# Gated MLP of a decoder layer: two leading pairs of plain products, and the last two down groups added in SBUF

## The chip, the cores and the metric

One core of a Trainium2 chip runs the kernel. The metric is the device time of one execution in microseconds (us), as a median over several executions. A change of about 0.2%, 5 us, is what a measurement of this kernel can tell from no change. An execution with the hardware profiler on gives the trace that is read here.

## The reference

The kernel computes one layer of a hybrid decoder on 2048 tokens of width 1024: three causal mixers with one input and one output projection, then a gated MLP, then a per-layer embedding with a gate, then a norm. The change touches the MLP alone:

```python
def conv_ffn(h, w_up, conv_w, w_down):          # h = rmsnorm(x): 2048 x 1024
    gu = causal_dwconv(h @ w_up, conv_w)        # w_up 1024 x 5632, taps of width 3
    g, u = jnp.split(gu, 2, axis=-1)            # 2 x 2816
    return (jax.nn.silu(g) * u) @ w_down        # w_down 2816 x 1024

x = x + conv_ffn(rmsnorm(x, norm_ffn_gain[i]), ffn_w_up[i], ffn_conv_w[i], ffn_w_down[i])
```

## The kernel before

**Halves, chunks, pairs.** The tokens are worked in two halves (`hf`) of 1024, a half in two chunks of 512, which is the width of one matmul. Activations lie with channels on the 128 partitions and tokens along the free side. The 2816 gate and 2816 up channels make `NJ` = 22 pairs `j` of 128 + 128 channels. Every operand of a matmul is split into a high and a low part (`split`, line 253: ACT copies the high part with rounding, DVE subtracts it from the source), and one product of a weight block with an activation block takes three matmuls (`mm3`, line 261: high x high, high x low, low x high; lines 262, 263, 264 of the profile).

**Products.** `prod` (line 847) multiplies one weight quarter (128 output channels, half of the input channels, so four blocks) with one activation set `X[i]`: 4 x 3 = 12 matmuls of 512 columns. `X[1]` and `X[2]` are the lower and the upper half of the channels of chunk 0, `X[3]` the upper half of chunk 1, `X[5]` chunk 1 minus chunk 0 of the lower half, and `X[6]`, `X[7]`, `X[4]` further differences. With them a pair (gate and up, two chunks, two channel halves: eight plain products) is had from seven products in the manner of Strassen and Winograd; its weights are sums of quarters that `up_jobs` (line 152) forms on DVE. `h2_first` (line 777) makes `X[1]` and `X[2]`, `h2_second` (line 786) the others, in steps between which products stand; eight of its subtractions run on POOL (lines 803 and 808).

**The lead.** `up_first` (line 881) works pair 0 with eight plain products, because the sums for the others aren't there yet: gate and up with `X[1]`, then `X[2]`, then `X[5]` and `X[3]`. The last four go to the two halves of one PSUM tile, `pbc`, of two banks. `up(j)` (line 919) works each further pair with seven products, and in between finishes pair `j - 1`: the depthwise convolution of width 3 (`conv`, line 399: one ACT operation for the first tap, a DVE step for each further one), silu, the multiplication (`gu_mul`) and the split of the result (`gu_split`).

**Down.** `GROUPS` (line 99) holds ten groups of two pairs and then pairs 20 and 21 alone. `down_pair` (line 950) multiplies a group of two with its down weights, six matmuls to a tile, copies the result out of PSUM on ACT (line 961) and adds it to `xd` in DRAM by an accumulating transfer of POOL's queue (line 962). After the last such group `x` is loaded from `xd` (line 1003). `down_last` (line 966) works pair 20 and then pair 21: three matmuls to a tile of 128 channels and one chunk, and DVE adds the tile into `x` in SBUF (line 974); for pair 21 the sum is split at once (`xsplit`, line 947) for the gate products that follow. Pair 21's silu, last product, convolution and multiplication are issued ahead of pair 20's tiles, its split after the sixth.

**What sets the order.** Weights are split in the order of `wlist` (lines 209 to 226), some jobs ahead of their use (`w_get`, line 240; `w_mlp`, line 250). A scheduler then orders the instructions of each engine; an engine works its queue in that order and waits where an operand isn't there. Its dependencies go by whole tiles: a write to one half of a tile waits for a read of the other half. ACT and DVE share the work of all splits, so that a split can stand behind work that waits for something else. PSUM has four tiles of one bank (`sm`) and two of two banks (`mm`).

## Time and profile before

| | us |
|---|---|
| median of 3 runs | 2551.55 (2551.5 to 2554.44) |
| the profiled execution | 2548.32 |
| its span, first to last instruction | 2546.5 |
| PE busy in it | 2454.9 (96%) |
| DVE busy | 1613.4 (63%) |
| ACT busy | 1310.7 (51%) |
| POOL busy | 237.2 (9%) |

The profile names a group of instructions by its line, engine and operation, and by the tiles that it writes and reads: `pbc<-h,wt` is a matmul that writes the tile `pbc` from an activation tile `h` and a weight tile `wt`. An idle time stands with what ended it (`<-`). PE is the matmuls, PEld the loading of weights into the array, which runs beside them; PEclk is the clock granted to TensorE as a share of its full 2.4 GHz. A table of windows gives for each its limits, its length, the busy time and (x) the count of PE, PEld, DVE, ACT and POOL, then PEclk, the busy share of the DMA engines and GB/s. `pa`, `pb`, `pc` and `pbc` are the PSUM tiles of the up products, `pdn` those of the down products, `zg` and `zu` gate and up before the convolution, `gu` behind it, `ahi` and `alo` the split activation, `wt` a split weight.

The first half's MLP lies from about 465 to 1168 us of the span, the second half's from about 1715 to 2412 us.

### The profile page before, as it was taken

How to read it: one execution, taken by the hardware profiler on the slowest of the kernel's cores; microseconds unless marked ns; L12 is line 12 of the kernel's file. 1: busy time of each engine (PE TensorE's matmuls, PEld its weight loads, DVE VectorE, ACT ScalarE, POOL GpSimd, SP SyncE). 2: the span in 40 equal slices, each digit the busy share in tenths (PEclk: the TensorE clock that was granted, in tenths of full speed). 3: DMA queues.
4: the chain of work that ended last, by engine and by line, in shares of the span. 5: the costliest groups of instructions: out<-in, count | busy, mean ns of one | idle time of the engine just before them, and what ended most of it. 6: DMA issues, size and time to landing. Idle time of an engine off the chain costs nothing. (4 is left out here: it accounts for less than half of the span.)

```text
span 2546.5 us, 30816 instructions
## 1 busy us (share of the span) xinstructions
PE 2454.9 (96%) x12004; PEld 2020.1 (79%) x12004; DVE 1613.4 (63%) x2384; ACT 1310.7 (51%) x1778; POOL 237.2 (9%) x278
## 2 busy tenths in 40 slices
PE   6999999899999999999999999997999999999998
PEld 4887788678888888887888887785888888888788
DVE  6666565685556566558666656567666666655776
ACT  5444884365555545555344457634555555555453
POOL 2000001201111111110110000012111111111100
PEclk9999999899999999999999999998999999999999
DMA  3101114346565555573421111251555555556642
GB/s 136 42 26 34 42 58 164 122 120 138 132 137 135 140 124 124 127 195 116 149 92 34 34 34 54 79 189 39 124 129 136 133 125 128 133 130 136 177 149 92
DMA packets 121170, 280.71 MB, mean 110 GB/s; under 512 B 11840, under 2 KB 42176, under 8 KB 121024
## 3 DMA queue, kind: packets, MB, share of 16 engines
q0 software_dynamic: 31360, 113.26, 21.3%
q1 hardware_dynamic: 88656, 164.30, 19.9%
q8 instruction: 94, 1.54, 0.2%
q10 hardware_dynamic: 1008, 1.18, 0.2%
q14 instruction: 52, 0.43, 0.1%
HBM read 178.03 MB, written 100.66 MB: 109 GB/s over the span
## 5 line engine op out<-in xcount | busy, mean ns | idle before, releaser
L262 PE MATMUL pz<-h,wh 128*128 128x512 f32 x768 | 306.3, 399 | 9.5 <-ACT h L255 9.5
L263 PE MATMUL pz<-h,wh 128*128 128x512 f32 x768 | 302.0, 394 | 1.2 <-DVE h L256 0.8
L264 PE MATMUL pz<-h,wl 128*128 128x512 f32 x768 | 300.6, 392 | 0.0
L262 PE MATMUL pdn<-ahi,wt 128*128 128x512 f32 x704 | 277.7, 394 | 12.6 <-DVE x L974 11.0
L264 PE MATMUL pa<-h,wt 128*128 128x512 f32 x704 | 276.5, 393 | 6.8 <-DVE wt L256 6.8
L262 PE MATMUL pa<-h,wt 128*128 128x512 f32 x704 | 276.3, 393 | 3.3 <-ACT wt L255 1.8
L263 PE MATMUL pdn<-alo,wt 128*128 128x512 f32 x704 | 275.8, 392 | 0.0
L264 PE MATMUL pdn<-ahi,wt 128*128 128x512 f32 x704 | 275.6, 392 | 0.0
L263 PE MATMUL pa<-h,wt 128*128 128x512 f32 x704 | 275.6, 391 | 0.0
L961 ACT ACTIVATE st<-pdn 128x1024 f32<-128x1024 f32 x160 | 164.0, 1026 | 210.5 <-PE pdn L264 189.9
L256 DVE TENSOR_TENSOR wt<-s,wt 128x512 fp32r<-128x512 f32 x168 | 114.1, 688 | 218.0 <-ACT wt L255 217.8
L962 POOL DMA_DIRECT2D xd<-st x160 | 136.9, 856 | 1087.4 <-ACT st L961 1084.3
L262 PEld LDWEIGHTS pz<-h,wh 128*128 128x128 f32 x768 | 144.8, 189 | 40.7 <-ACT h L255 10.7
L263 PEld LDWEIGHTS pz<-h,wh 128*128 128x128 f32 x768 | 144.8, 189 | 33.0 <-DVE h L256 4.1
L262 PEld LDWEIGHTS pdn<-ahi,wt 128*128 128x128 f32 x704 | 133.2, 189 | 45.6 <-DVE x L974 13.9
L264 PEld LDWEIGHTS pz<-h,wl 128*128 128x128 f32 x768 | 144.8, 189 | 30.1 <-issue 0.3
L256 DVE TENSOR_TENSOR wl<-wr,wh 128x1024 fp32r<-128x1024 f32 x120 | 146.2, 1227 | 35.1 <-ACT wh L255 34.7
L264 PEld LDWEIGHTS pa<-h,wt 128*128 128x128 f32 x704 | 133.3, 189 | 35.3 <-DVE wt L256 7.7
L262 PEld LDWEIGHTS pa<-h,wt 128*128 128x128 f32 x704 | 133.1, 189 | 33.0 <-ACT wt L255 2.7
L264 PEld LDWEIGHTS pdn<-ahi,wt 128*128 128x128 f32 x704 | 133.2, 189 | 28.0
L263 PEld LDWEIGHTS pa<-h,wt 128*128 128x128 f32 x704 | 133.1, 189 | 27.6
L263 PEld LDWEIGHTS pdn<-alo,wt 128*128 128x128 f32 x704 | 133.3, 189 | 27.1
(271 smaller groups left out, 5170.0 us busy)
## 6 DMA issues: line engine op xcount, KB each, us to landing
xd<-st POOLq DMA_DIRECT2D x160, 512.0 KB, 6.1
wr<-in_w_up SPq DMA_DIRECT2D x176, 256.0 KB, 4.1
wr<-in_w_in SPq DMA_DIRECT2D x48, 512.0 KB, 3.7
q<-in_w_down SPq DMA_DIRECT2D x88, 256.0 KB, 3.4
wr<-in_w_pg SPq DMA_DIRECT2D x40, 512.0 KB, 4.5
wr<-in_w_out SPq DMA_DIRECT2D x32, 512.0 KB, 3.8
q<-in_w_up SPq DMA_DIRECT2D x42, 256.0 KB, 3.0
xr<-in_xT POOLq DMA_DIRECT2D x32, 256.0 KB, 3.9
```

The source lines that it names most:

```text
L256: last_split[:] = i, (eng or nc.vector).tensor_tensor(lo, src, hi.bitcast(F32), op=SUB)
L262: MM(ps, wk[0], rk[0], start=start, stop=False, **kw)
L263: MM(ps, wk[0], rk[1], start=False, stop=False, **kw)
L264: MM(ps, wk[1], rk[0], start=False, stop=stop, **kw)
L961: ACT(st, ps, AF.Copy)
L962: nc.gpsimd.dma_start(xd[m], st, accum_op=ADD)
```

## The change

Pair 1 is worked like pair 0, with eight plain products (`FIRST` = 2). The products of both are ordered by activation set: four with `X[1]`, four with `X[2]`, four with `X[5]`, four with `X[3]`; `w_get` orders their weights so. Pair 1's sums with `X[1]` and `X[2]` go to the two halves of a tile `pbc`, and each pair's sums with `X[5]` and `X[3]` to a tile of their own. `up` begins with pair 2 and there has no `X[4]` product of pair 1 to do. Pair 0's convolutions, silu, multiplication and split stand in `up_first`. POOL's eight subtractions per half go to DVE.

The groups are now eleven, all of two pairs. The first nine accumulate in DRAM as before; pairs 18 and 19 and pairs 20 and 21 go through `down_last` behind the last product, with six matmuls to a tile and the add into `x` on DVE. Pair 21's silu, convolution, multiplication and split are steps between the tiles of the group ahead of it. `x` is loaded from `xd` ahead of the last product, when nine groups have accumulated in place of ten.

```diff
@@ -96,7 +96,8 @@
     def ftile(name, dt=F32):
         return pools["ff"].tile([P, TH], dt, tag="ff", name=nm(name))
 
-    GROUPS = [[j, j + 1] for j in range(0, NJ - 2, 2)] + [[NJ - 2], [NJ - 1]]
+    GROUPS = [[j, j + 1] for j in range(0, NJ, 2)]
+    FIRST = 2
 
     def ple_chunks(last):
 
@@ -176,11 +177,11 @@
             TT(t[:, QS[1]], raws[a][:, QS[0]], raws[a][:, QS[1]], op=SUB)
             return one(t[:, QS[1]])
 
-        if j == 0:
-            return [(("f", hf, 0), load0, lambda: one(raws[a][:, QS[0]])),
-                    (("f", hf, 1), None, lambda: one(raws[a][:, QS[1]])),
-                    (("f", hf, 2), load1, lambda: one(raws[b][:, QS[1]])),
-                    (("f", hf, 3), None, lambda: one(raws[b][:, QS[0]]))]
+        if j < FIRST:
+            return [(("f", hf, j, 0), load0, lambda: one(raws[a][:, QS[0]])),
+                    (("f", hf, j, 1), None, lambda: one(raws[a][:, QS[1]])),
+                    (("f", hf, j, 2), load1, lambda: one(raws[b][:, QS[1]])),
+                    (("f", hf, j, 3), None, lambda: one(raws[b][:, QS[0]]))]
         return [((1, hf, j), load0, lambda: one(raws[a][:, QS[0]])),
                 ((5, hf, j), load1, s1),
                 ((6, hf, j), None, lambda: one(raws[s][:, QS[1]])),
@@ -210,12 +211,14 @@
     for hf in range(NH):
         wlist += [(("in", hf, m), lambda m=m: whole(kc(w_in[m]), t4)) for m in IN_UNITS]
         wlist += [(("out", hf, c, m), lambda m=m: whole(kc(w_out[m]), t4)) for c in range(NC) for m in range(KD)]
-        for j in range(NJ):
+        firsts = [up_jobs(hf, j) for j in range(FIRST)]
+        wlist += [job for i in (0, 2) for jobs in firsts for job in jobs[i : i + 2]]
+        for j in range(FIRST, NJ):
             jobs = up_jobs(hf, j)
-            if j > 1:
+            if j > FIRST:
                 jobs.insert(2, last_job(hf, j - 1))
             wlist += jobs
-            if j % 2 == 0 and j:
+            if j % 2 == 0 and j < NJ - 2:
                 wlist += down_jobs(hf, j // 2 - 1)
         wlist.append(last_job(hf, NJ - 1))
         for gi in range(len(GROUPS) - 2, len(GROUPS)):
@@ -800,15 +803,16 @@
             for q in range(KQ):
 
                 TT(h0[q], h1[KQ + q], h0[q], op=SUB)
-                nc.gpsimd.tensor_tensor(h1[q], h1[KQ + q], h1[q], op=SUB)
                 X[6][q] = split_chunk(h0[q], "h")
             yield
             for q in range(KQ):
 
-                nc.gpsimd.tensor_tensor(h0[KQ + q], h0[KQ + q], h0[q], op=SUB)
+                TT(h1[q], h1[KQ + q], h1[q], op=SUB)
                 X[7][q] = split_chunk(h1[q], "h")
             yield
             for q in range(KQ):
+
+                TT(h0[KQ + q], h0[KQ + q], h0[q], op=SUB)
                 X[4][q] = split_chunk(h0[KQ + q], "h")
 
         norms = [Norm(), Norm()]
@@ -880,34 +884,51 @@
 
         def up_first():
 
-            w0, w1 = w_get("f", hf, 0), w_get("f", hf, 1)
-            A, A2, BC = ps1(name="pa"), ps1(name="pa"), ps2("pbc")
-            zg, zu = ftile("zg"), ftile("zu")
-            prod(A, w0, X[1], True, False)
-            ACT(zg[:, C1], A, AF.Copy)
-            norms[1].rstd()
-            prod(A2, w1, X[1], True, False)
-            ACT(zu[:, C1], A2, AF.Copy)
-            h2 = h2_second(norms[1].bcast())
+            pairs = range(FIRST)
+            w = {}
+            sums0 = [[ps1(name="pa"), ps1(name="pa")], None]
+            for j in pairs:
+                zs[j, 0], zs[j, 1] = ftile("zg"), ftile("zu")
+            for j in pairs:
+                if j:
+                    t = ps2("pbc")
+                    sums0[j] = [t[:, C0], t[:, C1]]
+                for i in range(2):
+                    w[j, i] = w_get("f", hf, j, i)
+                    prod(sums0[j][i], w[j, i], X[1], True, False)
+                    ACT(zs[j, i][:, C1], sums0[j][i], AF.Copy)
+                    if j == 0 and i == 0:
+                        norms[1].rstd()
+                    if j == 0 and i == 1:
+                        h2 = h2_second(norms[1].bcast())
+                        next(h2)
+            for j in pairs:
+                for i in range(2):
+                    w[j, 2 + i] = w_get("f", hf, j, 2 + i, ahead=min(2, 3 - 2 * j - i))
+                    prod(sums0[j][i], w[j, 2 + i], X[2], False, True)
+                    ACT(zs[j, i][:, C0], sums0[j][i], AF.Copy)
+                next(h2)
+
+            sums1 = []
+            for j in pairs:
+                t = ps2("pbc")
+                sums1.append([t[:, C0], t[:, C1]])
+                for i in range(2):
+                    prod(sums1[j][i], w[j, i], X[5], True, False)
             next(h2)
-            w2 = w_get("f", hf, 2, ahead=1)
-            prod(A, w2, X[2], False, True)
-            ACT(zg[:, C0], A, AF.Copy)
-            next(h2)
-            w3 = w_get("f", hf, 3, ahead=0)
-            prod(A2, w3, X[2], False, True)
-            ACT(zu[:, C0], A2, AF.Copy)
-
-            prod(BC[:, C0], w0, X[5], True, False)
-            prod(BC[:, C1], w1, X[5], True, False)
-            next(h2)
-            prod(BC[:, C0], w2, X[3], False, True)
-            TT(zg[:, C1], zg[:, C1], BC[:, C0], op=ADD)
-            prod(BC[:, C1], w3, X[3], False, True)
-            TT(zu[:, C1], zu[:, C1], BC[:, C1], op=ADD)
-            zs[0, 0], zs[0, 1] = zg, zu
-            g_conv(0)
-            run(h2)
+            for j in pairs:
+                for i in range(2):
+                    prod(sums1[j][i], w[j, 2 + i], X[3], False, True)
+                    TT(zs[j, i][:, C1], zs[j, i][:, C1], sums1[j][i], op=ADD)
+                if j == 0:
+                    g_conv(0)
+                    u_conv(0)
+                    g_silu(0)
+                    gu_mul(0)
+                    gu_split(0)
+                    run(h2)
+                else:
+                    g_conv(1)
 
         banks = {}
 
@@ -922,11 +943,11 @@
             zg, zu = zs[j, 0], zs[j, 1] = ftile("zg"), ftile("zu")
             prod(A, w_mlp(1, hf, j), X[1], True, False)
             ACT(zg[:, C0], A, AF.Copy)
-            if j % 2 == 0 or j == 1:
+            if j % 2 == 0 or j == NJ - 1:
                 g_silu(j - 1)
             prod(B, w_mlp(5, hf, j), X[5], True, False)
             ACT(zu[:, C1], B, AF.Copy)
-            if j > 1:
+            if j > FIRST:
                 last_prod(j - 1)
             u_conv(j - 1)
             prod(A, w_mlp(6, hf, j), X[6], False, False)
@@ -965,17 +986,29 @@
 
         def down_last(gi, todo=None):
 
-            j = GROUPS[gi][0]
-            w = [w_mlp("d", hf, gi, i) for i in range(2)]
+            js = GROUPS[gi]
+            final = gi == len(GROUPS) - 1
+
+            def tile(m, c, w):
+                ps = ps1(name="pdn")
+                for i, j in enumerate(js):
+                    mm3(ps, wsl(hsl(w), m % 2 * 2 + i), [a[:, cks(c)] for a in acts[j]], i == 0, i == 1)
+                TT(x[m][:, cks(c)], x[m][:, cks(c)], ps, op=ADD)
+
+            if not final:
+                for m in range(KD):
+                    if m % 2 == 0:
+                        w = w_mlp("d", hf, gi, m // 2)
+                    for c in range(NC):
+                        tile(m, c, w)
+                    if todo:
+                        next(todo, None)
+                return
+            w = [w_mlp("d", hf, gi, i) for i in range(KD // 2)]
             for c in range(NC):
                 for m in range(KD):
-                    ps = ps1(name="pdn")
-                    mm3(ps, wsl(hsl(w[m // 4]), m % 4), [a[:, cks(c)] for a in acts[j]], True, True)
-                    TT(x[m][:, cks(c)], x[m][:, cks(c)], ps, op=ADD)
-                    if gi == len(GROUPS) - 1:
-                        xsplit(c, m)
-                    if todo and c == 0 and m == 5:
-                        todo()
+                    tile(m, c, w[m // 2])
+                    xsplit(c, m)
 
         def stats_steps():
             for c in range(NC):
@@ -991,22 +1024,29 @@
         up_first()
         nstats = []
         stats = iter(()) if last else stats_steps()
-        for j in range(1, NJ):
+        for j in range(FIRST, NJ):
             up(j)
-            if j > 1:
-                next(stats, None)
-            if j % 2 == 0:
+            next(stats, None)
+            if j % 2 == 0 and j < NJ - 2:
                 down_pair(j // 2 - 1, lambda: g_silu(j))
         run(stats)
+        j = NJ - 1
         for m in range(KD):
             x[m] = t4("x")
             nc.gpsimd.dma_start(x[m], xd[m])
-        j = NJ - 1
-        g_silu(j)
+
+        def last_steps():
+            g_silu(j)
+            yield
+            u_conv(j)
+            yield
+            yield
+            gu_mul(j)
+            yield
+            gu_split(j)
+
         last_prod(j)
-        u_conv(j)
-        gu_mul(j)
-        down_last(len(GROUPS) - 2, lambda: gu_split(j))
+        down_last(len(GROUPS) - 2, last_steps())
         down_last(len(GROUPS) - 1)
         ff.release()
 
```

How the change moves instructions is shown at three places, as they stand in each engine's queue. The number behind a name tells tiles of one kind apart; line numbers of the change are its own.

PE, first half, where the `X[5]` sums come in. Before, the `X[2]` products (`pa` with `wt_3518`) are done and `pbc_3523` begins:

```order
L264 MATMUL pa_3522<-h_3424,wt_3518 128x512
L262 MATMUL pbc_3523<-h_3576,wt_3444 128x512
L263 MATMUL pbc_3523<-h_3576,wt_3444 128x512
L264 MATMUL pbc_3523<-h_3576,wt_3444 128x512
L262 MATMUL pbc_3523<-h_3581,wt_3444 128x512
```

Now, from the sixth matmul on `X[5]` on (`pbc_3724`; `h_3577`, `h_3582` and `h_3587` are its first blocks), with `wt_3599`, `wt_3615` and `wt_3634` the weights for `X[2]` (`h_3363`):

```order
L267 MATMUL pbc_3724<-h_3582,wt_3444 128x512
L265 MATMUL pbc_3724<-h_3587,wt_3444 128x512
L265 MATMUL pa_3512<-h_3363,wt_3599 128x512
L266 MATMUL pa_3512<-h_3363,wt_3599 128x512
L266 MATMUL pbc_3724<-h_3587,wt_3444 128x512
L265 MATMUL pa_3513<-h_3363,wt_3615 128x512
L266 MATMUL pa_3513<-h_3363,wt_3615 128x512
L265 MATMUL pbc_3595<-h_3363,wt_3634 128x512
L267 MATMUL pa_3512<-h_3363,wt_3599 128x512
```

The last row is the first that takes the low part of a weight for `X[2]`; seven matmuls on `X[5]` stand ahead of the `X[2]` products, the rest of them behind.

ACT, first half, at the first weight of the first pair with seven products. Before, that is `wt_3746`, and the silu of pair 0 stands behind it:

```order
L255 ACTIVATE h_3733<-h_485_3270 128x512
L255 ACTIVATE h_3736<-h_485_3270 128x512
L255 ACTIVATE wt_3746<-wr_3743 128x512
L255 ACTIVATE wt_3755<-s_3752 128x512
L255 ACTIVATE wt_3758<-s_3752 128x512
L255 ACTIVATE wt_3761<-wr_3749 128x512
L867 ACT_TABLE_LOAD
L867 ACTIVATE gu_3706<-gu_3706 128x1024
```

Now it is `wt_3886`, for pair 2:

```order
L871 ACTIVATE gu_3816<-gu_3816 128x1024
L406 ACTIVATE gu_3821<-zu_3515,vt 128x1024
L406 ACTIVATE gu_3874<-zg_3516,vt 128x1024
L306 ACTIVATE sq_5844<-xs_5842 128x512
L306 ACTIVATE sq_6139<-xs_6137 128x512
L258 ACTIVATE ahi_3828<-gu_3816 128x1024
L258 ACTIVATE h_3833<-h_484_3269 128x512
L258 ACTIVATE h_3837<-h_484_3269 128x512
L258 ACTIVATE h_3841<-h_485_3270 128x512
L258 ACTIVATE h_3845<-h_485_3270 128x512
L258 ACTIVATE wt_3886<-wr_3883 128x512
```

The same place of DVE's queue in the change, where the multiplication of pair 0 (`gu_3816`) and the low parts stand:

```order
L922 TENSOR_TENSOR zu_3517<-zu_3517,pbc_3749 128x512
L410 SCALAR_TENSOR_TENSOR gu_3821<-zu_3515,vt,gu_3821 128x1022
L410 SCALAR_TENSOR_TENSOR gu_3874<-zg_3516,vt,gu_3874 128x1023
L878 TENSOR_TENSOR gu_3816<-gu_3816,gu_3821 128x1024
L410 SCALAR_TENSOR_TENSOR gu_3874<-zg_3516,vt,gu_3874 128x1022
L259 TENSOR_TENSOR alo_3829<-gu_3816,ahi_3828 128x1024
L259 TENSOR_TENSOR h_3833<-h_484_3269,h_3833 128x512
L259 TENSOR_TENSOR h_3837<-h_484_3269,h_3837 128x512
L259 TENSOR_TENSOR h_3841<-h_485_3270,h_3841 128x512
L259 TENSOR_TENSOR h_3845<-h_485_3270,h_3845 128x512
L259 TENSOR_TENSOR wt_3886<-wr_3883,wt_3886 128x512
```

The silu, multiplication and split of pair 0 moved ahead of the first weight of the next pair; the first row reads the last product of the lead, pair 1's `pbc_3749`.

PE, first half, the last down group. Before, two tiles of pair 21:

```order
L262 MATMUL pdn_8534<-ahi_8468,wt_8407 128x512
L263 MATMUL pdn_8534<-alo_8469,wt_8407 128x512
L264 MATMUL pdn_8534<-ahi_8468,wt_8407 128x512
L262 MATMUL pdn_8542<-ahi_8468,wt_8407 128x512
L263 MATMUL pdn_8542<-alo_8469,wt_8407 128x512
L264 MATMUL pdn_8542<-ahi_8468,wt_8407 128x512
```

Now, one tile of pairs 20 (`ahi_8193`) and 21 (`ahi_8372`), and the first matmul of the next:

```order
L265 MATMUL pdn_8448<-ahi_8193,wt_8315 128x512
L266 MATMUL pdn_8448<-alo_8194,wt_8315 128x512
L267 MATMUL pdn_8448<-ahi_8193,wt_8315 128x512
L265 MATMUL pdn_8448<-ahi_8372,wt_8315 128x512
L266 MATMUL pdn_8448<-alo_8373,wt_8315 128x512
L267 MATMUL pdn_8448<-ahi_8372,wt_8315 128x512
L265 MATMUL pdn_8459<-ahi_8193,wt_8315 128x512
```

A tile that DVE adds is now behind six matmuls in place of three.

## Rows read from the trace of the kernel before

**Rows 1.** The page, span and engine shares of the whole run.

```profile
span 2546.5 us, 30816 instructions
...
PE 2454.9 (96%) x12004; PEld 2020.1 (79%) x12004; DVE 1613.4 (63%) x2384; ACT 1310.7 (51%) x1778; POOL 237.2 (9%) x278
```

**Rows 2.** Waits of PE: line, what it waited for, us, times, longest.

```profile
PE pdn L262 <- DVE x L974: 11.0, 4, 4.9
...
PE pbc L262 <- DVE zg L905: 8.5, 2, 6.7
```

**Rows 3.** Windows: a steady stretch, the two leads, the two ends.

```profile
600.00:1090.00 490.00, 489.97 (x2167) 404.89 (x2166) 291.45 (x407) 257.27 (x350) 54.74 (x64) 1.00 0.57 132
487.00:556.10 69.10, 56.53 (x205) 42.86 (x205) 65.75 (x88) 39.80 (x64) 12.66 (x8) 0.85 0.24 77
1736.40:1805.10 68.70, 54.10 (x205) 40.97 (x205) 61.61 (x85) 35.68 (x54) 13.43 (x8) 0.88 0.13 41
1120.00:1180.00 60.00, 54.68 (x226) 43.40 (x226) 48.70 (x69) 30.06 (x41) 5.99 (x10) 0.94 0.53 166
2370.00:2432.00 62.00, 56.10 (x237) 45.30 (x235) 55.48 (x81) 30.50 (x42) 4.29 (x8) 0.94 0.42 145
```

**Rows 4.** Windows with the lower granted clock, same columns.

```profile
490.80:497.60 6.80, 5.92 (x13) 4.36 (x14) 6.80 (x9) 2.85 (x6) 3.78 (x3) 0.50 0.25 77
...
1767.50:1774.20 6.70, 6.09 (x14) 4.79 (x15) 3.92 (x7) 1.42 (x3) 0.00 (x0) 0.50 0.30 99
2395.60:2402.20 6.60, 4.14 (x10) 3.25 (x11) 6.53 (x9) 2.60 (x3) 0.00 (x0) 0.50 0.23 79
```

**Rows 5.** Timeline of PE, leads of both halves: start, duration, what, [idle before].

```profile
508.09 0.79 PE L262 MATMUL pbc<-h,wt 128*128 128x512 f32 x1 [1.78 <-DVE zg L905]
...
1756.97 0.79 PE L262 MATMUL pbc<-h,wt 128*128 128x512 f32 x1 [6.69 <-DVE zg L905]
...
1768.11 0.80 PE L264 MATMUL pa<-h,wt 128*128 128x512 f32 x1 [3.66 <-DVE wt L256]
```

**Rows 6.** Timeline of PE, end of the second half's MLP.

```profile
2398.06 0.80 PE L262 MATMUL pdn<-ahi,wt 128*128 128x512 f32 x1 [4.87 <-DVE x L974]
...
2409.43 0.50 PE L262 MATMUL pdn<-ahi,wt 128*128 128x512 f32 x1 [0.93 <-DVE x L974]
```

**Rows 7.** Timeline of DVE, lead of the first half.

```profile
491.73 1.28 DVE L256 TENSOR_TENSOR h<-h,h 128x512 fp32r<-128x512 f32 x2
...
495.58 3.46 DVE L256 TENSOR_TENSOR h<-h,h 128x512 fp32r<-128x512 f32 x2
...
512.61 0.69 DVE L907 TENSOR_TENSOR zu<-zu,pbc 128x512 f32<-128x512 f32 x1
...
514.41 4.29 DVE L256 TENSOR_TENSOR h<-h,h 128x512 fp32r<-128x512 f32 x7
...
528.80 1.28 DVE L407 SCALAR_TENSOR_TENSOR gu<-zu,vt,gu 128x1023 f32<-128x1023 f32 x1
...
532.43 1.22 DVE L874 TENSOR_TENSOR gu<-gu,gu 128x1024 f32<-128x1024 f32 x1
```

**Rows 8.** Timeline of DVE, lead of the second half.

```profile
1741.40 0.69 DVE L256 TENSOR_TENSOR h<-h,h 128x512 fp32r<-128x512 f32 x1
```

**Rows 9.** Timeline of ACT, lead of the first half and pair 2.

```profile
509.57 3.73 ACT L255 ACTIVATE h<-h 128x512 fp32r<-128x512 f32 x7
...
533.68 1.06 ACT L255 ACTIVATE ahi<-gu 128x1024 fp32r<-128x1024 f32 x1 [1.30 <-DVE gu L874]
534.64 0.61 ACT L255 ACTIVATE wt<-s 128x512 fp32r<-128x512 f32 x1
```

**Rows 10.** Timeline of DVE, end of the first half's MLP.

```profile
1162.89 2.35 DVE L256 TENSOR_TENSOR wl<-wr,wh 128x1024 fp32r<-128x1024 f32 x2
...
1166.96 1.89 DVE L256 TENSOR_TENSOR xs<-x,xs 128x512 fp32r<-128x512 f32 x3
1168.76 1.88 DVE L974 TENSOR_TENSOR x<-x,pdn 128x512 f32<-128x512 f32 x3
```

## Prediction

> **What bounds the kernel now.** I read the page first: TensorE (PE) is busy 96% of a span of 2546.5 us [rows 1], so the time is the PE's matmuls plus the stretches in which it stands still or runs slowly. A steady stretch gives the pitch: 2167 matmuls of 512 columns in 490 us, 0.2265 us each [rows 3]; nothing can be won there. So I looked for the stretches that the change touches and counted what they hold against that pitch. In the lead of the MLP, from the first product with the X5 sums to the first down product, 204 matmuls (the window's 205 holds one begun earlier) are worth 46.2 us and take 69.1 us in the first half, 68.7 us in the second: 22.9 and 22.5 us lost [rows 3]. At the end of the MLP, 225 of the 226 matmuls in a window of 60 us are worth 51.0 us and 235 in one of 62 us 53.2 us: 9.0 and 8.8 us lost [rows 3]. That is 63 us in all, the most that this change can work on.
>
> The waits of PE say what ends the idle time. At the end it is the add of a down product into x on VectorE (DVE), 11.0 us [rows 2], one wait of 4.87 us in the second half [rows 6]. In the lead the largest is the add that reads one half of the two-bank tile pbc, 8.5 us [rows 2], 6.69 us of it in the second half [rows 5]. The third loss is the clock: behind these waits the granted clock is 0.50, the lower level of 1.2 GHz, for stretches such as the three of 6.6 to 6.8 us shown [rows 4], and a matmul there costs twice the pitch. A wait thus also costs time behind it. PE resumes at 1768.11 and 2398.06 [rows 5, 6], in stretches that stay low up to 1774.2 and 2402.2 [rows 4]: 6.1 and 4.1 us of work at half rate, mean 5.1, so about 2.5 us lost per wait.
>
> **The lead, part by part.** Pair 1 gets eight products in place of seven: 12 more matmuls per half, +2.7 us; 216 are now worth 48.9 us. Three pair-1 weight sums and splits go, which only frees DVE and ScalarE (ACT).
>
> First wait, kept. The order puts seven matmuls on X5 (ten in the second half) ahead of the X2 products, and X2's weights are split only behind the last X5 split. Up to the first low part of a weight PE has 13 matmuls (14). In the first half it starts them at about 486.8; DVE ends its last X5 split at 491.73 + 1.28 = 493.0 [rows 7], and one split more (seven in 4.29 us: 0.60 each [rows 7]) makes 493.7 with the handoff. Loss 6.9 - 13 x 0.2265 = 4.0 us. Up to here the work is that of before, so the low clock from 490.8 to 497.6 [rows 4] stays: 3.9 us of work at half rate, 1.95 us. Second half: from 1736.2 to 1741.40 + 0.69 + 0.60 = 1742.7 [rows 8], 6.5 - 14 x 0.2265 = 3.3 us; there the clock held before, and I count nothing.
>
> Then PE has 83 matmuls on X2 and X5 before the first one on X3, some 19 us. DVE needs about 10 us for what X3 wants: four weight splits, four scalings, two subtractions, four splits. So the X3 waits of before vanish. The eight subtractions taken from POOL cost DVE 8 x 0.60 = 4.8 us per half, but two DVE splits beside POOL's subtractions took 3.46 us in place of 1.2 [rows 7]; that stretching goes. The rest of DVE's queue up to the first add of an X3 product is some 23 operations, 14 us: it gets there about when that product is done, 516 to 517 us. I cost the move at nothing; the cover is thin, and the first rival prices its absence.
>
> The half-tile wait stays in part: the last X3 product of pair 1 writes one half of a tile whose other half DVE must have read. PE now has another product between, so only the tail of an add and a convolution step is left. The nearest row, 1.78 us [rows 5], is the upper end, nothing the lower; I take 1.5 and 1.0 us. The Trainium skill (Perfetto Trace Analysis, Optimizing Tensor Performance, Matmuls) says that groups in different PSUM banks let the evacuation of one overlap the matmuls of the next; by that the two halves, a bank each, need not wait, and the sum would be 2.5 us lower. The trace disagrees for this code, 6.69 us [rows 5]: the dependency is on the tile.
>
> New wait, the heart of this sum. The order shows the first weight of pair 2 behind the high part of pair 0's activation and four X4 splits on ACT. That activation needs the whole of pair 0: once the last X3 product is done, DVE adds it (0.69), does two convolution steps (1.28 each; in the second half the queue has them elsewhere) and the multiplication (1.22) [rows 7]; then ACT makes the activation's high part (1.06), four splits (seven in 3.73: 0.53 each) and the weight (0.61) [rows 9]. Nothing else is left for PE. First half, with consecutive DVE steps at 1.20 and 0.4 us of handoffs: 0.4 + 0.6 + 1.2 + 1.2 + 1.2 + 1.06 + 2.1 + 0.6 = 8.4 us; second half without the two steps 6.0 us. The low part, behind DVE's own queue, comes about 0.9 us later: 9.3 and 6.9 us. Then the low clock, unseen for this place: 0 if it holds, 3.4 if all 6.8 us lie on work, 2.5 taken as above.
>
> Sum of the losses: 4.0 + 1.95 + 1.5 + 9.3 + 2.5 = 19.3 us, so the first down product starts at 486.8 + 48.9 + 19.3 = 555.0 against 556.1: **-1.1 us**. Second half: 3.3 + 1.0 + 6.9 + 2.5 = 13.7, 1736.2 + 48.9 + 13.7 = 1798.8 against 1805.1: **-6.3 us**. What the eight products win in the lead they nearly give back behind pair 0.
>
> **The end, part by part.** The matmuls stay the same in number. Before, the last two groups come three matmuls to a tile: a tile takes PE 0.68 us and DVE an add of 0.63 (three in 1.88), in the last pass also a split of 0.63 [rows 10]: 1.26 us, so DVE bound it, and pair 21's convolutions and splits stood in the same queue. Now a tile takes six matmuls, 1.36 us, the same DVE work: in the first pass half of DVE is free for pair 21, whose 21.7 us of cover replace 10.9; in the last pass 1.26 is below 1.36. The x loads no longer wait for the accumulations of pairs 18 and 19, which end in PSUM and are added straight; 8 evacuations on ACT and 8 stores per half go, off PE's path. What remains I bound by nothing and by the smallest wait there now, 0.93 us [rows 6], and take the upper. **-8.1 us** and **-7.9 us**.
>
> Sum: -1.1 - 6.3 - 8.1 - 7.9 = **-23.4 us**. The profiled execution took 2548.3 us (span 2546.5 and 1.8 around it), which gives 2524.9; the median of the runs shown is 2551.55, 3.2 us above it, and on that I forecast 2528 us. About 0.2%, 5 us, is what a measurement can tell from no change.
>
> **Rivals.**
> A: DVE becomes the bound of the lead. For it: DVE is busy 65.8 of 69.1 us there [rows 3] and meets PE with a margin of a microsecond. Against: the stretching beside POOL goes. If all eight subtractions fall on the path, 2 x 4.8 = 9.6 us come back: 2538 us. The Trainium skill (Perfetto Trace Analysis, Optimizing Scalar/DVE Operations) speaks for this rival: work may be offloaded to GpSimd where DVE is saturated, and the change does the reverse; it adds that the two share a read port so that it might not help, and the 3.46 us bears that out. Chance 0.12.
> B: the last pass is still DVE's. The weight splits of the next stage stand in that queue (two in 2.35 us [rows 10]); with three of them DVE's 16 tiles take 16 x 1.26 + 3.5 = 23.7 us against 21.7: 2 us per half, 2532 us. Chance 0.10.
> C, on the other side: the clock stays low between the two waits of the lead and behind them. Each matmul more at the low level costs 0.2265 us; from (23.4 + 5) / 2 / 0.2265 = 63 per half the kernel is slower, and with all 135 from 497.6 us up to the new wait it is 2528 + 2 x 135 x 0.2265 = 2589 us. For it: the new wait is the longest in the MLP. Against: the low stretches of waits up to 6.7 us end by themselves [rows 4, 5]. Chance 0.04.
> D: the new chain takes twice as long (DVE late, ACT held by statistics): 2 x 8 more, 2544, and with two further low stretches no change, 2549 us. Chance 0.05.
>
> **How the numbers follow.** Forecast 0.69, A 0.12, B 0.10, D 0.05, C 0.04. Faster 0.69 + 0.12 + 0.10 = 0.91, same 0.05, slower 0.04. The low end takes no low clock (-6.95), no half-tile wait (-2.5) and no rest at the end (-1.8): 2517. The high end holds A (2538) and the low clock at 3.4 behind each wait: 2540. C and D are left out.
>
> **What would show it.** Right: PE waits for pair 2's first weight split once per half, 6 to 9 us, with a granted clock of 0.50 behind it; the 6.69 us wait and the add waits of the last groups are gone; no DVE split of h takes over 1.2 us. Wrong: end losses over 3 us per half (B), a wait of the first X3 add for DVE's own queue (A), low stretches over 7 us (C), a lead of more than 69 us.

## The result, and the profile after

The changed kernel takes 2520.97 us, the median of four runs (2518.2 to 2523.93), against 2551.53 us for four runs of the kernel before (2547.7 to 2554.44) beside it: ratio 0.988, 95% interval 0.9864 to 0.9896. The forecast was 2528 us, in a range of 2517 to 2540. It was faster, as forecast, by about 30.6 us by the medians where the working gave 23.4.

The profiled execution after the change took 2518.2 us, with a span of 2516.4 us. The line of its page with the busy times, and its waits of PE, which answer to [rows 1, 2]:

```profile
PE 2445.4 (97%) x12028; PEld 2017.6 (80%) x12028; DVE 1599.2 (64%) x2384; ACT 1292.0 (51%) x1756; POOL 197.4 (8%) x246
```

```profile
PE pa L265 <- ACT wt L258: 13.8, 3, 8.0
...
PE pbc L265 <- DVE zg L922: 2.0, 2, 1.2
```

The columns are what PE waited for, us in all, times, longest. The waits of a down product for an add into x (11.0 us before) do not occur at all; the wait for the half tile of pbc has gone from 8.5 to 2.0 us; and the wait for a split weight on ACT, 13.8 us, is the new one that the prediction was built around.

The windows of the two leads and the two ends after the change answer to [rows 3] (length, busy us and count of each engine, granted clock of PE, DMA share, GB/s):

```profile
484.00:552.30 68.30, 56.54 (x219) 44.10 (x218) 61.81 (x94) 40.11 (x63) 0.00 (x0) 0.88 0.25 79
1721.90:1784.70 62.80, 54.58 (x220) 42.10 (x219) 56.41 (x86) 33.82 (x52) 0.00 (x0) 0.95 0.13 40
1100.00:1160.40 60.40, 60.40 (x267) 49.72 (x267) 52.55 (x74) 27.18 (x39) 2.85 (x6) 1.00 0.42 149
2326.60:2388.70 62.10, 62.00 (x274) 51.00 (x274) 54.30 (x82) 29.38 (x43) 4.19 (x8) 1.00 0.43 153
```

The two lead windows also hold two or three matmuls that stand ahead of the lead. Counted as before, from the first product with the X5 sums (484.26 and 1722.36 us) to the first down product (552.26 and 1784.69), a lead holds 216 matmuls, worth 48.9 us at 0.2265 us each, and takes 68.0 and 62.3 us: 19.1 and 13.4 us are lost, where 22.9 and 22.5 were lost before. Both end windows lose nothing: 267 matmuls are worth 60.5 us and stand in 60.4, at a granted clock of 1.00, where 9.0 and 8.8 us were lost before.

The chain behind the new wait: PE's timeline in both halves (start, us, what, [idle before, releaser]), then DVE's and ACT's in the first half.

```profile
521.68 0.50 PE L265 MATMUL pbc<-h,wt 128*128 128x512 f32 x1 [1.19 <-DVE zg L922]
532.69 0.80 PE L265 MATMUL pa<-h,wt 128*128 128x512 f32 x1 [7.99 <-ACT wt L258]
...
1756.47 0.50 PE L265 MATMUL pbc<-h,wt 128*128 128x512 f32 x1 [0.78 <-DVE zg L922]
1765.09 0.79 PE L265 MATMUL pa<-h,wt 128*128 128x512 f32 x1 [5.60 <-ACT wt L258]
1768.22 0.79 PE L267 MATMUL pa<-h,wt 128*128 128x512 f32 x1 [0.20 <-DVE wt L259]
```

```profile
524.74 0.69 DVE L922 TENSOR_TENSOR zu<-zu,pbc 128x512 f32<-128x512 f32 x1 [0.60 <-PE pbc L267]
525.34 1.28 DVE L410 SCALAR_TENSOR_TENSOR gu<-zu,vt,gu 128x1022 f32<-128x1022 f32 x1
526.53 1.28 DVE L410 SCALAR_TENSOR_TENSOR gu<-zg,vt,gu 128x1023 f32<-128x1023 f32 x1
527.73 1.22 DVE L878 TENSOR_TENSOR gu<-gu,gu 128x1024 f32<-128x1024 f32 x1
```

```profile
528.98 1.06 ACT L258 ACTIVATE ahi<-gu 128x1024 fp32r<-128x1024 f32 x1 [3.31 <-DVE gu L878]
529.95 2.17 ACT L258 ACTIVATE h<-h 128x512 fp32r<-128x512 f32 x4
532.02 0.61 ACT L258 ACTIVATE wt<-wr 128x512 fp32r<-128x512 f32 x1
```

These are the terms of the sum one after another: the add, two convolution steps and the multiplication on DVE, then the high part of the activation, four splits of X4 and pair 2's first weight on ACT, and PE starts 0.67 us after that weight was begun. Behind both waits the clock is at its lower level, as in the windows of [rows 4]:

```profile
532.60:538.80 6.20, 6.09 (x14) 4.31 (x15) 6.20 (x12) 3.81 (x7) 0.00 (x0) 0.50 0.15 48
...
1764.40:1771.10 6.70, 5.81 (x13) 4.08 (x14) 6.67 (x12) 3.69 (x7) 0.00 (x0) 0.50 0.00 0
```

### The profile page after: what moved, and what is told of

The parts are those of the page before. It is cut to its first block, busy times and chain, and to the rows that moved or that the text cites. A ratio compares the mean times of both kernels' runs of the same rounds, so it can differ in the third digit from the quotient of the medians.

```text
span 2516.4 us, 30778 instructions
## 1 busy us (share of the span) xinstructions
PE 2445.4 (97%) x12028; PEld 2017.6 (80%) x12028; DVE 1599.2 (64%) x2384; ACT 1292.0 (51%) x1756; POOL 197.4 (8%) x246
## 5 line engine op out<-in xcount | busy, mean ns | idle before, releaser
L265 PE MATMUL pa<-h,wt 128*128 128x512 f32 x672 | 265.1, 394 | 14.0 <-ACT wt L258 13.8
L266 PE MATMUL pa<-h,wt 128*128 128x512 f32 x672 | 264.0, 393 | 0.0
L267 PE MATMUL pa<-h,wt 128*128 128x512 f32 x672 | 263.7, 393 | 0.2 <-DVE wt L259 0.2
L982 ACT ACTIVATE st<-pdn 128x1024 f32<-128x1024 f32 x144 | 147.9, 1027 | 194.2 <-PE pdn L267 185.4
L259 DVE TENSOR_TENSOR wt<-s,wt 128x512 fp32r<-128x512 f32 x160 | 108.4, 688 | 192.9 <-ACT wt L258 192.9
L983 POOL DMA_DIRECT2D xd<-st x144 | 123.1, 855 | 1034.4 <-ACT st L982 1033.7
L265 PEld LDWEIGHTS pa<-h,wt 128*128 128x128 f32 x672 | 127.7, 190 | 42.7 <-ACT wt L258 15.5
L267 PEld LDWEIGHTS pa<-h,wt 128*128 128x128 f32 x672 | 127.5, 190 | 28.3 <-DVE wt L259 1.7
L266 PEld LDWEIGHTS pa<-h,wt 128*128 128x128 f32 x672 | 127.7, 190 | 26.4
```

The costliest lines, as they stand in the source:

```text
L259: last_split[:] = i, (eng or nc.vector).tensor_tensor(lo, src, hi.bitcast(F32), op=SUB)
L265: MM(ps, wk[0], rk[0], start=start, stop=False, **kw)
L266: MM(ps, wk[0], rk[1], start=False, stop=False, **kw)
L267: MM(ps, wk[1], rk[0], start=False, stop=stop, **kw)
L982: ACT(st, ps, AF.Copy)
L983: nc.gpsimd.dma_start(xd[m], st, accum_op=ADD)
```

## Where the 30.1 us of the profiled executions lie

The starts of the same matmuls in the two traces, by stage (us; a minus is a gain). The lead begins with the first product with the X5 sums, which starts at 487.04 and 1736.42 us before and at 484.26 and 1722.36 after:

| stage | forecast | first half | second half |
|---|---|---|---|
| out projection, ahead of the lead | 0 | -3.0 | -0.6 |
| lead, up to the first down product | -1.1 / -6.3 | -1.1 | -6.4 |
| last two down groups | -8.1 / -7.9 | -8.8 | -8.4 |
| other stretches behind the first down product | 0 | -0.8 | -1.3 |

The first stage of the run adds 0.2 us. The term that was not there at all is the out projection. These are its windows in the first half and the last wait of PE in it, the kernel before, then the changed one:

```profile
461.00:483.90 22.90, 21.06 (x91) 16.68 (x90) 6.34 (x14) 3.76 (x8) 2.71 (x5) 0.93 0.51 172
470.40:473.80 3.40, 3.40 (x9) 2.62 (x8) 0.69 (x1) 0.11 (x1) 0.89 (x2) 0.51 0.62 203
```

```profile
469.85 0.50 PE L262 MATMUL po<-ys,wh 128*128 128x512 f32 x1 [1.15 <-DVE x L765]
```

```profile
460.50:480.90 20.40, 19.58 (x93) 15.83 (x91) 5.14 (x12) 3.85 (x8) 2.71 (x5) 1.00 0.55 192
470.00:474.00 4.00, 4.00 (x19) 3.29 (x19) 0.00 (x0) 0.00 (x0) 0.00 (x0) 1.00 0.73 239
```

```profile
468.32 0.50 PE L265 MATMUL po<-ys,wh 128*128 128x512 f32 x1 [0.39 <-DVE x L768]
```

Before, PE waited twice at the end of the out projection (0.69 and 1.15 us) and then ran nine matmuls at the lower clock. Now a product of pair 1 with X1, whose weights are ready, stands on both sides of the last out products, PE waits 0.39 us, and the clock holds. In every trace here the first 48 up matmuls of a half fall into this stretch; from the first to the 49th the first half takes 22.4 to 23.4 us in the three kernels with one leading pair and 19.5 to 20.5 us in the eight with two.

## Experiments

Each was timed in several runs beside runs of the kernel before; the ratio is to those, with its 95% interval. The edits are cut to the lines that matter; those of the end alone and of the two tiles stand against the kernel before, the others against the changed kernel or the run that they build on. A stretch of about ten matmuls at half pace near 38 us, which costs some 3 us, is in four of the eleven traces and not in the others, whatever the edit, so profiles are compared stage by stage, not by their whole span.

**The end alone.** The lead of before, POOL's subtractions kept; the changed groups:

```diff
-    GROUPS = [[j, j + 1] for j in range(0, NJ - 2, 2)] + [[NJ - 2], [NJ - 1]]
+    GROUPS = [[j, j + 1] for j in range(0, NJ, 2)]
+    FIRST = 1
```

> The end of the change alone (eleven groups of two pairs, the last two added in SBUF with six matmuls to a tile); lead and POOL's subtractions as before. Theory (the parts add up, and the end was worth more than the 8.1 + 7.9 us forecast): 16 to 20 us below the kernel before, 2532 to 2535 us, no PE wait on an add into x of 0.9 us or more in the end; the lead keeps its 69 us. Rival (the end wins only because the lead shifted the work that runs into it): 8 us or less, 2543 us or more, with waits of a down product for x still in the trace.

Measured: 2532.15 us, ratio 0.9935 (0.9923 to 0.9947), 16.3 us faster. The end windows:

```profile
1104.40:1164.60 60.20, 60.20 (x267) 49.53 (x266) 52.58 (x75) 27.31 (x39) 2.73 (x6) 1.00 0.42 149
2337.60:2399.60 62.00, 61.91 (x274) 50.95 (x273) 54.34 (x82) 29.41 (x43) 4.29 (x8) 1.00 0.43 153
```

No loss is left in them, and no wait for an add into x; the lead is that of before to 0.3 us. The end's gain is its own. Which part of the edit makes it (six matmuls to a tile, the earlier load of x, pair 21's steps between tiles) no run separates.

**The lead alone.** Two pairs with eight products and the subtractions on DVE; the end as before.

```diff
-            js = GROUPS[gi]
+            j = GROUPS[gi][0]
...
-                    tile(m, c, w[m // 2])
+                    mm3(ps, wsl(hsl(w[m // 4]), m % 4), [a[:, cks(c)] for a in acts[j]], True, True)
```

> The lead of the change alone (two pairs with eight products, subtractions on DVE); the end as before. Theory (the lead itself gives 0.8 and 6.1 us, and the products of pair 1 that now stand ahead of the lead's first wait fill 3 to 4 us of idle or slow PE there): 8 to 12 us below the kernel before, 2540 to 2544 us, with PE waits for the first weight split of pair 2 of about 8 and 6 us. Rival (the gain ahead of the lead is chance of one profile): 7 us or less, 2545 us.

Measured: 2538.95 us, ratio 0.9959 (0.9947 to 0.9972), 9.5 us faster. By stage, from the first X5 product on as above: out projection -3.1 and -0.3, lead -0.8 and -7.2, then -1.3 and -1.2 in the rest, with the end's 4.9 us waits still there. So the gain ahead of the lead repeats with the lead's edit and only with it (the end alone has 0.0 there in the first half), and the small gains in the rest belong to this part too; where each of those comes from was not traced. The two parts add up to 25.8 us by the medians, 1.06% by the ratios, against 1.2% for the whole change; the difference is within the intervals.

**The subtractions back on POOL.**

```diff
-                TT(h1[q], h1[KQ + q], h1[q], op=SUB)
+                nc.gpsimd.tensor_tensor(h1[q], h1[KQ + q], h1[q], op=SUB)
...
-                TT(h0[KQ + q], h0[KQ + q], h0[q], op=SUB)
+                nc.gpsimd.tensor_tensor(h0[KQ + q], h0[KQ + q], h0[q], op=SUB)
```

> The changed kernel with its eight subtractions per half given back to POOL. Theory (the move to DVE costs nothing, since DVE's splits stretch beside POOL's subtractions, 3.46 us for two in place of 1.2): 0 to 5 us slower than the changed kernel, 2521 to 2526 us, with splits of h of over 1.2 us back in the trace. Rival (DVE is the bound of the lead and POOL would relieve it): up to 9.6 us faster, 2511 to 2516 us, and the wait for pair 2's first weight split gets shorter by as much.

Measured: 2530.82 us, ratio 0.9925 (0.9912 to 0.9938), some 11 us above the changed kernel by the two ratios. Between the two profiled executions lie 12.6 us, some 4 ahead of the first lead (most of it the stretch near 38 us) and 4.0 and 4.1 in the two leads. Neither theory gave so much. DVE in this kernel's second lead, POOL beside it, ACT, and PE:

```profile
1739.66 1.41 DVE L805 TENSOR_TENSOR h<-h,h 128x512 f32<-128x512 f32 x1
1741.00 3.47 DVE L259 TENSOR_TENSOR h<-h,h 128x512 fp32r<-128x512 f32 x2
...
1747.02 4.64 DVE L259 TENSOR_TENSOR h<-h,h 128x512 fp32r<-128x512 f32 x4
```

```profile
1739.24 2.99 POOL L810 TENSOR_TENSOR h<-h,h 128x512 f32<-128x512 f32 x2 [17.06 <-DVE h L778]
```

```profile
1745.16 1.81 ACT L258 ACTIVATE h<-h 128x512 fp32r<-128x512 f32 x3 [2.65 <-DVE h L778]
...
1747.67 0.58 ACT L909 ACTIVATE zg<-pbc 128x512 f32<-128x512 f32 x1
```

```profile
1748.30 0.50 PE L265 MATMUL pbc<-h,wt 128*128 128x512 f32 x1 [2.57 <-ACT zg L909]
```

And the same DVE line in the changed kernel (its first lead), where POOL is idle:

```profile
499.46 0.69 DVE L805 TENSOR_TENSOR h<-h,h 128x512 f32<-128x512 f32 x1
500.06 2.49 DVE L259 TENSOR_TENSOR h<-h,h 128x512 fp32r<-128x512 f32 x4
```

Beside a subtraction on POOL (1.5 us each) a subtraction on DVE takes 1.41 in place of 0.69 us and four splits 4.64 in place of 2.49. ACT then gets its next split late (it stands 2.65 us for DVE), and behind that split stands the copy that frees a tile for PE: a new wait of 2.57 us, eight matmuls at the low clock after it. Taking eight subtractions onto DVE therefore costs nothing here; it gains about 4 us per half.

This also says where the lead's gain comes from. With the subtractions on POOL, two pairs of plain products make leads of 72.0 and 66.4 us, against 69.1 and 68.7 with one pair before and 68.0 and 62.3 with two pairs and the subtractions on DVE. The second pair alone would have made the first lead longer by 2.9 us and the second shorter by 2.3; so the gain in the two leads needs the move off POOL. The move with a single leading pair was not run.

**Two tiles for the half-tile wait**, in the kernel before:

```diff
-            A, A2, BC = ps1(name="pa"), ps1(name="pa"), ps2("pbc")
+            A, A2 = ps1(name="pa"), ps1(name="pa")
...
+            BC = [ps1(name="pbc"), ps1(name="pbc")]
```

> The kernel before with the two halves of pair 0's two-bank tile as two tiles of one bank each, so that the second X3 product no longer waits for DVE's add out of the other half. Theory (the wait of 6.69 us is where PE meets DVE's queue, not its cause: the add and pair 1's weight splits stand behind the same DVE work, so the wait moves to the next weight): within 4 us of the kernel before, the wait for the add gone and the wait for pair 1's weight split longer by as much. Rival (the wait is the price of the shared tile): 7 to 12 us faster, 2.2 and 6.9 us and the low clock behind them gone.

Measured: 2546.96 us, ratio 0.9985 (0.9976 to 0.9994), about 3.8 us faster by the ratio. In the second half the wait for the add (6.69 us, [rows 5]) is gone and PE stands at pair 1's weight:

```profile
1766.85 0.80 PE L262 MATMUL pa<-h,wt 128*128 128x512 f32 x1 [11.20 <-ACT wt L255]
1771.41 0.79 PE L264 MATMUL pa<-h,wt 128*128 128x512 f32 x1 [1.64 <-DVE wt L256]
```

The two waits of the second half before, 6.69 and 3.66 us, are now 11.20 and 1.64. The shared tile makes PE wait, but it was not what most of the time was lost to; DVE's queue was, as the theory had it: ACT gets to that weight behind splits that wait for DVE's subtractions, and these are slow beside POOL's. One of each, in the same place of the kernel before:

```profile
1749.42 1.76 DVE L802 TENSOR_TENSOR h<-h,h 128x512 f32<-128x512 f32 x1
```

```profile
1748.97 1.66 POOL L808 TENSOR_TENSOR h<-h,h 128x512 f32<-128x512 f32 x1 [0.63 <-DVE h L802]
```

**The activation of pair 0 later.** Its silu, multiplication and split are issued behind the first product of pair 2:

```diff
                     u_conv(0)
-                    g_silu(0)
-                    gu_mul(0)
-                    gu_split(0)
...
+            if j == FIRST:
+                g_silu(0)
+                gu_mul(0)
+                gu_split(0)
```

> The changed kernel with the activation of pair 0 (the silu, the multiplication and its split) issued behind the first product of pair 2 in place of ahead of it, so that the weights of pair 2 and the four X4 splits no longer stand behind pair 0's activation on ACT and DVE. Theory (the wait of 8.2 + 0.4 and 5.8 + 0.2 us is this order on ACT and DVE and nothing else, and the low clock behind it goes with it): 16 to 22 us below the changed kernel, 2499 to 2505 us, no PE wait of over 2 us between pair 1's last product and the first down product. Rival (DVE's or ACT's work as a whole binds there, so another wait takes its place): 5 us or less, 2516 us or more, with a new wait of similar size in the products of pair 2 or 3.

Measured: 2508.5 us, ratio 0.9839 (0.9825 to 0.9853), some 10 us below the changed kernel, short of the 16 expected. In both leads the new wait is gone, and the low clock behind it too. In the first half PE leads the changed kernel by 12.6 us behind the lead, but only by 4.0 us after two down groups. The waits of PE, its timeline and ACT's there:

```profile
PE pdn L265 <- ACT st L983: 5.4, 2, 2.7
```

```profile
559.00 0.50 PE L265 MATMUL pdn<-ahi,wt 128*128 128x512 f32 x1 [2.66 <-ACT st L983]
```

```profile
557.41 0.63 ACT L306 ACTIVATE sq<-xs 128x512 f32<-128x512 f32 x1 [4.92 <-DMA xs<-in_xT]
557.95 1.00 ACT L983 ACTIVATE st<-pdn 128x1024 f32<-128x1024 f32 x1
...
611.56 1.06 ACT L871 ACTIVATE gu<-gu 128x1024 f32<-128x1024 f32 x1 [3.20 <-DVE ftail L414]
```

The chain was the cause, as the theory had it, but 8.7 of the 12.6 us went into two new waits for a down tile, each with seven matmuls at the low clock. At the first, ACT stands at the squares of the next half's input until a load lands, and the copy that frees the tile is queued behind. At the second, the copies stand behind a silu that waits for DVE, and DVE had added squares of the same statistics four times in the 32 us before.

**The statistics later, first try.**

```diff
             up(j)
-            next(stats, None)
+            if j >= 6:
+                next(stats, None)
```

> The kernel with the late activation of pair 0, and the statistics of the second half's input started four pairs later (from pair 6). Theory (of the 12.6 us that PE wins in the lead of the first half, 8.7 go back at the first two down groups, where ACT stands 4.9 us for the load of that input ahead of the copy that frees a down tile, and DVE does its squares; two PE waits of 2.8 and 2.9 us with seven matmuls each at the low clock): without that load there the two waits shrink below 1 us, 5 to 9 us faster than with the activation late alone, about 2501 us. Rival (ACT and DVE have no slack there whatever they wait for): 2 us or less, the same two waits.

Measured: 2505.39 us, ratio 0.9827 (0.9813 to 0.9841), within the uncertainty of the run with the late activation alone, with the same two waits, of 2.64 and 2.73 us. But the edit did not do what it says: on ACT and on SP the squares and their loads kept their places, and the wait for the load stayed:

```profile
557.94 0.63 ACT L306 ACTIVATE sq<-xs 128x512 f32<-128x512 f32 x1 [4.91 <-DMA xs<-in_xT]
```

This run decides nothing between the theories.

**X2's weights earlier**, on top of that:

```diff
-                    w[j, i] = w_get("f", hf, j, i)
+                    w[j, i] = w_get("f", hf, j, i, ahead=4 if j == 0 and i == 1 else 2)
```

> The kernel of the late activation and late statistics, with the two weights of pair 0's X2 products split ahead of the X5 splits. Theory (the first wait of the lead, 3.4 us with 8 to 11 matmuls at the low clock behind it in the first half and 2.4 us in the second, is there since PE has no product but X5's to do until X2's weights are split): the X2 products fill it, 3 to 6 us in the first half and 2 in the second, 5 to 8 us in all, about 2494 us. Rival (what is split earlier delays the X5 and X3 splits by as much on DVE): 2 us or less, with a new wait in the X5 or X3 products.

Measured: 2503.52 us, ratio 0.9819 (0.9805 to 0.9833). That is 1.9 us below the run before, as little as the rival gave, but not by its mechanism: the first wait of the lead went and no wait of that size came in the X5 or X3 products; the longest wait for a down tile grew from 2.7 to 3.7 us. Of 5.3 us won in the first lead half are gone behind the two down groups and the rest by the end of that MLP. So the gain in the lead does not last while the statistics stand where they do.

**The statistics held back**, with the late activation and with the edit of the first try:

```diff
-                    n.add(s)
+                    with tc.issue_after(last_split[0].ins):
+                        n.add(s)
```

> The kernel with the late activation, and the squares of the second half's input on ACT held behind the split that stands ahead of them in the program, from pair 6 on (the run before it only wrote them later, and the order on ACT and SP stayed as it was). Theory (ACT's wait of 4.9 us for that load, ahead of the copy that frees a down tile, makes the PE waits of 2.8 and 2.9 us at the first two down groups): both waits below 1 us and no low clock there, 5 to 9 us faster than with the activation late alone, about 2499 us. Rival (ACT and DVE have no slack there): 2 us or less, the same two waits.

Measured: 2495.97 us, ratio 0.9779 (0.9764 to 0.9793), some 15 us below the late activation alone by the two ratios, 9.4 us between the profiled executions; 5 to 9 were expected. "The run before it" is the first try above. The stretch of the two down groups has no loss (500 matmuls are worth 113.2 us):

```profile
537.00:650.00 113.00, 113.00 (x500) 93.59 (x499) 68.76 (x96) 59.91 (x82) 13.70 (x16) 1.00 0.61 144
```

In the first half it gains 2.3 us in the lead on the late activation alone and 10.4 up to the end of the two down groups, and gives some 2.5 back later in that half. Neither of the two waits is left; the silu that waited at 611.56 starts at 600.18 and PE doesn't wait behind it. So the theory holds in that the statistics made both waits: the first by the load ahead of the copy, as it says. For the second the edit takes away the load and DVE's additions together, and no run tells them apart.

**Both, with X2's weights earlier.** The edit of the weights from above, on top of this one.

> The kernel of the run before with the two weights of pair 0's X2 products split ahead of the X5 splits. Theory (with the statistics out of the way the earlier weights fill the first wait of the lead and nothing takes its place): 4 to 8 us faster than the run before, about 2493 us, no PE wait of over 1 us between the out projection and the first down product. Rival (it only moves the wait to the down tiles, as it did with the statistics in place): 2 us or less.

Measured: 2489.71 us, ratio 0.976 (0.9746 to 0.9774), 6 us below the run before, as the theory had it, and some 30 us below the changed kernel: the fastest here. Its leads hold 216 matmuls, worth 48.9 us. These windows count them and begin 0.3 to 0.4 us behind the start of the first:

```profile
486.00:534.80 48.80, 48.80 (x216) 40.06 (x215) 48.45 (x73) 31.25 (x48) 0.00 (x0) 1.00 0.10 33
1703.70:1754.10 50.40, 49.43 (x216) 39.88 (x215) 49.91 (x78) 31.72 (x48) 0.00 (x0) 1.00 0.11 34
```

From the first start the leads take 49.2 and 50.8 us, so of the 22.9 and 22.5 us lost in the two leads before the change, 0.3 and 1.8 us are left.

## Why the prediction was right, and where not

**The lead.** Right in sum (-1.1 and -6.3 forecast, -1.1 and -6.4 measured), and nearly so in each term. Up to the first low part of a weight PE lost 4.9 and 3.1 us against 4.0 and 3.3; in the first half the clock fell within that stretch already, and the low matmuls behind it lost 1.2 us against 1.95. The half-tile wait was 1.19 and 0.78, against 1.5 and 1.0. The new wait was 7.99 us against 8.4, in the second half 5.60 against 6.0. From its end on, 13 matmuls took 6.1 us (6.2) in place of 2.9, the wait for the low part among them: 3.2 us (3.3) lost, against 3.4 for low part and clock together. The terms miss by up to 0.9 us and mostly cancel; that the sum comes out to 0.1 us is luck. That the wait is the order on ACT and DVE is shown by the late activation, which removes it. The statement that the eight products nearly give back what they win in the first half holds.

Two readings of the rows are a little off. The first X5 product starts at 487.04 and 1736.42 us, not at 486.8 and 1736.2, and 490 us for 2167 matmuls is 0.2261 us each, not 0.2265; neither moves a term by more than 0.3 us. A matmul at the low level is not worth two pitches: the starts lie 0.43 us apart in these stretches, so it costs 0.20 us more, not 0.2265.

**The half tile.** The prediction said that the dependency is on the tile, and the two one-bank tiles bear that out: the wait for the other half went. The forecast did not rest on how much two tiles are worth, and they are worth little: most of the wait moved to the next weight.

**The move from POOL.** "I cost the move at nothing" had the right reason and the wrong balance. The stretching beside POOL was put at one pair of splits; measured, it reaches DVE's subtractions and splits alike, and through ACT it reaches PE. Four subtractions of 1.75 us in the second lead of the kernel before showed it already. Left on POOL, the subtractions cost 4 us in each lead, 8.1 in all, more than the two leads gain together (7.5 us). Rival A, DVE as the bound of the lead, is refuted with its sign: the relief by POOL that it priced at 9.6 us would have been a loss. The Trainium skill (Perfetto Trace Analysis, Optimizing Scalar/DVE Operations) says that offloading to GPSIMD may make sense where DVE is saturated, and that it might not help because the two share a read port of SBUF; for these operations the measured 1.41 against 0.69 us speaks for the caution alone.

**The end.** Right in sum, and mis-sized by a little: -8.8 and -8.4 against -8.1 and -7.9. The rest of 0.93 us that was kept as an upper bound did not occur: PE is busy for all but 0.1 us of the two windows. Rival B, a last pass bound by DVE, did not happen. That the six matmuls to a tile are what did it fits the rows, but is argued: the edit changes the load of x and pair 21's place as well.

**What was missing.** The step that failed is the start of the count: the prediction begins at the first X5 product and puts whatever stands ahead of it at nothing ("Up to here the work is that of before"). The low clock that this sentence keeps did stay (0.50 from 487.8 to 494.6 us), but pair 1's X1 products run ahead of the lead, in the out projection, and gained 3.0 and 0.6 us where nothing was counted. With the ends (1.2 us more than forecast) and the small stretches behind the first down product (2.1 us, uncounted too) this makes the 6.7 us by which the profiled execution beat the sum, to 0.2 us. The prediction looked for what the eight products do inside the lead, and not for where else their first matmuls could stand.

**Clock and chain.** Rivals C and D did not happen: the low clock behind the new waits ended after 6 to 7 us, and the chain took the time of its rows.

## What to carry to other kernels

Work whose operands are ready early can pay wherever PE waits nearby, so look where its instructions land in the order, not only at the stage it belongs to. An offload to POOL is to be priced with what it does to DVE beside it, by a row with POOL busy and one with POOL idle. When a wait is removed, the next instruction in the same in-order queue decides how much of the gain is kept: here a statistic for the next half, urgent for nobody, held the copy that frees PE's tile.

## What was not expected of the hardware

A wait of the same length does not always bring the low clock. In two kernels the same down product was released after 2.73 us; behind it the one ran eight matmuls in 3.40 us at a granted clock of 0.51, the other fifteen at 1.00. The windows, of the statistics' first try and then of X2's weights earlier:

```profile
614.40:617.80 3.40, 3.40 (x8) 2.72 (x9) 0.69 (x1) 1.34 (x2) 1.72 (x2) 0.51 0.55 88
```

```profile
615.80:619.20 3.40, 3.38 (x15) 2.80 (x16) 0.69 (x1) 1.72 (x3) 1.72 (x2) 1.00 0.52 78
```

What PE did ahead differs a little between the two (in the second it had waited 0.85 us some 30 us earlier), and no run here tells whether that matters. The stretching of DVE beside POOL, two times for a subtraction, reaches more of DVE's work than the one pair of splits that the forecast had read.
